# Norming and shifting a feed-forward's input a second time, for its later chunks

## The chip, the cores and the metric

The kernel runs on one core of one Trainium2 chip. The metric is the device time of one execution in microseconds (us). Engines are named as in the profile: PE is TensorE's matmul and PEld its weight load, DVE is VectorE, ACT is ScalarE, POOL is GpSimd, SP is SyncE, which issues the DMAs. DVE and ACT work off their instructions in the order of the program.

## The reference

Two layers, each of three sublayers: a half-step feed-forward network (FFN), a token mixer (attention, Fourier, gMLP), a second half-step FFN. 384 token columns are held: 128 of a prompt and 256 of a sample, each group with its own conditioning vector. What matters here:

```python
def modulate(x, g, shift, scale):
    return rmsnorm(x, g) * (1 + scale) + shift
def swiglu(h, w_in, w_out):
    gate, up = jnp.split(h @ w_in, 2, axis=-1)
    return (jax.nn.silu(gate) * up) @ w_out
# in trunk_layer, for the FFNs 0 and 1:
h = modulate(x, npre[0], mod[:, :, 0], mod[:, :, 1])
x = x + 0.5 * mod[:, :, 2] * rmsnorm(swiglu(h, fw_in[0], fw_out[0]), npost[0])
# mod = silu(c) @ ada_w[l] + ada_b[l], one vector of 9 * 1024 per group (adaLN)
```

D_MODEL is 1024, the FFN's inner width 2816. All tensors are float32.

## The kernel before, in words

Activations lie transposed: 128 features on the partitions, 8 tiles (KT) of 384 columns (T). Every float32 product is made of three matmuls of rounded parts (`mm3`, L176 to L179): high weights with high input, high weights with low input, low weights with high input. Weights are streamed in pieces of 128x1024; ACT rounds a piece to its high part (`whi`, L132), DVE subtracts (`wlo`, L135), five pieces ahead (HOLD).

**An FFN's first product.** 44 *chunks* of 128 rows of `w_in` (22 gates, 22 ups, alternating) are each made by 24 matmuls: 8 input tiles by three. The first chunks of an FFN (6 in the first FFN, 4 in the others) run while the input arrives (`Enter.group`). The others run one after another in the loop at L521; I number these c0, c1, ... A gate and its up are a *pair*. The input is not normed before it is multiplied: the columns hold x times the gain, two more columns (T+2 = 386) hold the shift, and the norm `r` and the shift's share are applied to the result when a chunk leaves PSUM (`biased`, L430; `leave`, L500): per pair DVE copies two columns and multiplies 384 by r for the gate and again for the up, ACT applies Silu with the shift's share as bias on the two groups apart, DVE adds the other bias and multiplies (two instructions, L508), ACT rounds (`ahi`), and POOL subtracts (`alo`, L135).

**Order within the loop.** For each pair: `leave` of the pair before, then for each of its two chunks the split of a weight piece four chunks further on, the chunk's 24 matmuls, and a share of the adaLN products. The rounding of that piece on ACT waits until PE is done with the chunk before, whose buffer it takes.

**adaLN.** The vectors `mod` are made on DVE: one item of `ada_some` is two multiply-and-sum instructions over 1024 columns (L101) and gives 128 of them; 128 items in all. `plan` (L896) says how many of them lie in each FFN's first and second product; before, none lie in the mixes. `Enter.gain` (`A`, L217) of the next sublayer, made while the present one's second product still runs, needs the items of its gain.

**Between sublayers.** `Post.add` squares each finished tile on ACT, POOL adds the squares to `accy`, and PE's sum over partitions (L196) opens the next sublayer. `Enter.begin`, which needs `A`, stands ahead of the second to last of these squares in ACT's order. `Enter.restore` (L421) takes a reciprocal on DVE and brings x to its true scale: on POOL in the FFNs, on POOL and DVE in the mixes.

Of the kernel before, what the change touches and what calls it, by code (L numbers as in the profile page):

```python
# [5 lines left out]
F32 = mybir.dt.float32  # L6
# [6 lines left out]
P = 128  # L13
# [34 lines left out]
def model(nc, tc, a, o):  # L48
# [159 lines left out]
    class Enter:  # L208
# [220 lines left out]

        def biased(self, ps):  # L430
# [63 lines left out]
    def ffn(l, s, post, ada_in, ada_out, enter, after):  # L494
        ps = enter.group()
        with tc.tile_pool(name="ff", bufs=1) as fp:
# [3 lines left out]
            def leave(m, pg, pu):  # L500
                t, bg = enter.biased(pg)
                for j, b, e in RANGES:
                    nc.scalar.activation(t[:, b:e], t[:, b:e], AF.Silu, bias=bg[:, j:j + 1])  # L503
                up, bu = enter.biased(pu)

                def rest():
                    for j, b, e in RANGES:
                        nc.vector.scalar_tensor_tensor(  # L508
                            out=up[:, b:e], in0=up[:, b:e], scalar=bu[:, j:j + 1], in1=t[:, b:e],
                            op0=ALU.add, op1=ALU.mult)  # L510
                    split(ahi[:, m, :], alo[:, m, :], up, nc.gpsimd)

                return rest

            pairs = [(m, ps[2 * m], ps[2 * m + 1]) for m in range(len(ps) // 2)]
            leave(*pairs[0])()
            split_to(at[0] + HOLD - 1)
            for pair in pairs[1:-1]:
                leave(*pair)()
            first = len(pairs)  # L520
            for m in range(first, FT):  # L521
                rest = leave(*pairs[-1])
                for j in range(2):
                    w, = take(between=None if j else rest)
                    p = bank(px if len(ps) == FIRST and enter.post is None else pm)
                    products(p[:, :T + 2], w, enter.parts, range(KT))
                    ps.append(p)
                    if m < FT - REST:
                        ada_some(spread(ada_in, 2 * (m - first) + j, 2 * (FT - REST - first)))
                pairs.append((m, ps[-2], ps[-1]))  # L530
                if first < m <= first + KT:
                    enter.restore([m - first - 1])
            leave(*pairs[-1])()
# [19 lines left out]
    def mix(l, post, enter, after):  # L553
        ps = enter.group()
        with tc.tile_pool(name="mx", bufs=1) as mp, tc.tile_pool(name="m2", bufs=2) as m2:
# [322 lines left out]
            post = Post(l, 1)  # L878
            for i, p in enumerate(outs):
                products(p, w3[i], oparts, [7])  # L880
            enter.restore()
            for m in range(3, KT):
# [7 lines left out]
                outs.append(p)  # L890
                if m == KT - 2:
                    after(post, following)
# [101 lines left out]
```

## Time and profile before

| | |
|---|---|
| three timed runs, median (range) | 1541.15 us (1540.25 to 1542.49) |
| the profiled execution, its own time | 1538.58 us |
| its span | 1536.6 us, so 2.0 us lie around it |
| PE, PEld busy | 1467.3 us (95%), 1418.9 us (92%) |
| DVE, ACT, POOL busy | 1219.7 us (79%), 676.1 us (44%), 420.5 us (27%) |
| granted TensorE clock, mean | 0.991 |

The stages in order, from the span's start: layer 0's first FFN to 317.1 us, the mix to 490.6, the second FFN to 781.3; layer 1's first FFN to 1069.3, its mix to 1228.9, its second FFN to 1520.5, then the output. A matmul's record is longer than the distance from one to the next, since they overlap: rates are read by dividing a stretch by the matmuls in it. "Busy" for PE is therefore no measure of waiting; the idle time in brackets and the time per matmul are.

### The profile page before, as it was taken

How to read it: one execution, taken by the hardware profiler on the slowest of the kernel's cores; microseconds unless marked ns; L12 is line 12 of the kernel's file. 1: busy time of each engine (PE TensorE's matmuls, PEld its weight loads, DVE VectorE, ACT ScalarE, POOL GpSimd, SP SyncE). 2: the span in 40 equal slices, each digit the busy share in tenths (PEclk: the TensorE clock that was granted, in tenths of full speed). 3: DMA queues.
4: the chain of work that ended last, by engine and by line, in shares of the span. 5: the costliest groups of instructions: out<-in, count | busy, mean ns of one | idle time of the engine just before them, and what ended most of it. 6: DMA issues, size and time to landing. Idle time of an engine off the chain costs nothing.

```text
span 1536.6 us, 22588 instructions
## 1 busy us (share of the span) xinstructions
PE 1467.3 (95%) x8412; PEld 1418.9 (92%) x8412; DVE 1219.7 (79%) x2040; ACT 676.1 (44%) x1262; POOL 420.5 (27%) x293
## 2 busy tenths in 40 slices
PE   9999999979889999999999999999989989999996
PEld 7999989978778999999989999999877979999995
DVE  4799999996776899999988999887777789666323
ACT  4533334346655533334344333433667654433331
POOL 1211111124534333121132422111454343311012
PEclk9999999999999999999999999999999999999998
DMA  9566667844333255667835556676244315544441
GB/s 370 192 197 194 203 198 241 260 138 140 97 97 117 87 174 181 200 194 241 259 118 167 177 193 194 204 221 189 91 122 121 102 44 182 174 134 123 119 118 41
DMA packets 87005, 254.12 MB, mean 165 GB/s; under 512 B 21616, under 2 KB 26224, under 8 KB 85872
## 3 DMA queue, kind: packets, MB, share of 16 engines
q1 hardware_dynamic: 86896, 252.68, 51.9%
q8 instruction: 66, 1.08, 0.3%
q14 instruction: 43, 0.35, 0.1%
HBM read 250.03 MB, written 2.62 MB: 164 GB/s over the span
## 4 chain that ended last, share of the span: by engine, by line
PE 56%; DVE 28%; ACT 7%; issue 6%; DMA 2%; POOL 1%; SPq 0%; DVEq 0%; ACTq 0%; POOLq 0%
PE ps L179 17%; PE ps L178 17%; PE ps L177 17%; DVE junk L101 8%; DVE wlo L135 7%; ACT whi L132 3%; DVE hlo L234 2%; DVE x L270 2%; DVE x L268 2%; DVE t L435 1%; DVE p L756 1%; DMA rpb<-in_rpb_dram 1%; PE ps L196 1%; DMA raw<-in_ffn_w_in_dram 1%; ACT t L503 1%
## 5 line engine op out<-in xcount | busy, mean ns | idle before, releaser
L178 PE MATMUL ps<-hlo,whi 128*128 128x386 f32 (+1 forms) x1700 | 579.3, 341 | 11.4 <-DVE hlo L234 10.6
L177 PE MATMUL ps<-hhi,whi 128*128 128x386 f32 (+1 forms) x1700 | 587.1, 345 | 0.8 <-ACT whi L132 0.8
L179 PE MATMUL ps<-hhi,wlo 128*128 128x386 f32 (+1 forms) x1700 | 579.0, 341 | 2.9 <-DVE wlo L135 2.9
L135 DVE TENSOR_TENSOR wlo<-raw,whi 128x1024 fp32r<-128x1024 f32 (+1 forms) x298 | 389.5, 1311 | 171.1 <-ACT whi L132 165.3
L132 ACT CAST whi<-raw 128x1024 fp32r<-128x1024 f32 x324 | 329.9, 1024 | 220.4 <-PE ps L178 144.9
L101 DVE CUSTOM_DVE_ANT_0 junk<-adaw,cb,adab 128x1024 bf16<-128x1024 f32 x256 | 367.4, 1435 | 4.6
L178 PEld LDWEIGHTS ps<-hlo,whi 128*128 128x128 f32 x1700 | 322.8, 190 | 18.7 <-DVE hlo L234 16.8
L177 PEld LDWEIGHTS ps<-hhi,whi 128*128 128x128 f32 x1700 | 322.5, 190 | 6.8 <-issue 2.5
L179 PEld LDWEIGHTS ps<-hhi,wlo 128*128 128x128 f32 x1700 | 322.0, 189 | 6.2 <-DVE wlo L135 6.0
L135 POOL TENSOR_TENSOR alo<-t,ahi 128x384 fp32r<-128x384 f32 x88 | 135.6, 1541 | 513.9 <-ACT ahi L132 513.9
L177 PE MATMUL ps<-ahi,whi 128*128 128x384 f32 x768 | 257.7, 336 | 0.7 <-ACT whi L132 0.7
L179 PE MATMUL ps<-ahi,wlo 128*128 128x384 f32 x768 | 257.1, 335 | 0.6 <-DVE wlo L135 0.6
L178 PE MATMUL ps<-alo,whi 128*128 128x384 f32 x768 | 257.1, 335 | 0.0
L503 ACT ACTIVATE t<-t,b 128x128 f32<-128x128 f32 (+1 forms) x176 | 70.6, 448 | 389.8 <-DVE t L435 389.8
L177 PEld LDWEIGHTS ps<-ahi,whi 128*128 128x128 f32 x768 | 144.3, 188 | 1.3 <-ACT whi L132 1.0
L179 PEld LDWEIGHTS ps<-ahi,wlo 128*128 128x128 f32 x768 | 144.3, 188 | 1.0 <-DVE wlo L135 1.0
L178 PEld LDWEIGHTS ps<-alo,whi 128*128 128x128 f32 x768 | 144.3, 188 | 0.0
L457 POOL TENSOR_TENSOR accy<-accy,sqy 128x384 f32<-128x384 f32 x36 | 54.2, 1506 | 311.0 <-ACT sqy L455 310.9
L435 DVE TENSOR_TENSOR t<-ps,r 128x384 f32<-128x384 f32 x212 | 114.7, 548 | 0.2
L135 POOL TENSOR_TENSOR wlo<-raw,whi 128x1024 fp32r<-128x1024 f32 x26 | 63.2, 2433 | 50.4 <-ACT whi L132 36.2
L508 DVE SCALAR_TENSOR_TENSOR t<-t,b 128x128 f32<-128x128 f32 (+1 forms) x176 | 66.2, 417 | 9.2
L245 POOL TENSOR_TENSOR accx<-accx,sqx 128x384 f32<-128x384 f32 x42 | 46.5, 1107 | 70.3 <-ACT sqx L244 69.0
(167 smaller groups left out, 1146.8 us busy)
## 6 DMA issues: line engine op xcount, KB each, us to landing
raw<-in_ffn_w_in_dram SPq DMA_DIRECT2D x176, 512.0 KB, 3.4
adaw<-in_ada_w_dram SPq DMA_DIRECT2D x128, 512.0 KB, 3.6
raw<-in_ffn_w_out_dram SPq DMA_DIRECT2D x64, 512.0 KB, 3.8
raw<-in_w_in_dram SPq DMA_DIRECT2D x36, 512.0 KB, 4.0
raw<-in_ffn_w_out_dram SPq DMA_DIRECT2D x32, 384.0 KB, 3.7
piece<-in_ada_first_dram SPq DMA_DIRECT2D x8, 1024.0 KB, 8.7
raw<-in_w_out_dram SPq DMA_DIRECT2D x16, 512.0 KB, 3.3
rpb<-in_rpb_dram SPq DMA_DIRECT2D x32, 96.0 KB, 6.3
```

The costliest lines, as they stand in the source:

```text
L101: nc.vector.tensor_tensor_reduce(out=junk, in0=w, in1=cb[:, j, :], scale=1.0, scalar=adab[:, l, b, f:f + 1], op0=ALU.mult, op1=ALU.add, ac ...
L132: nc.scalar.copy(hi, src)
L135: (eng or nc.vector).tensor_tensor(out=lo, in0=src, in1=hi, op=ALU.subtract)
L177: nc.tensor.matmul(ps, whi, hhi, start=start, stop=False)
L178: nc.tensor.matmul(ps, whi, hlo, start=False, stop=False)
L179: nc.tensor.matmul(ps, wlo, hhi, start=False, stop=stop)
L234: nc.vector.scalar_tensor_tensor(out=self.hlo[:, k, b:e], in0=x[:, k, b:e], scalar=self.A[:, k, j:j + 1], in1=self.hhi[:, k, b:e], op0=ALU ...
L245: nc.gpsimd.tensor_tensor(out=self.acc, in0=self.acc, in1=sq, op=ALU.add)
L435: nc.vector.tensor_tensor(out=t, in0=ps[:, :T], in1=self.r, op=ALU.mult)
L457: nc.gpsimd.tensor_tensor(out=self.acc, in0=self.acc, in1=sq, op=ALU.add)
L503: nc.scalar.activation(t[:, b:e], t[:, b:e], AF.Silu, bias=bg[:, j:j + 1])
L508: nc.vector.scalar_tensor_tensor(out=up[:, b:e], in0=up[:, b:e], scalar=bu[:, j:j + 1], in1=t[:, b:e], op0=ALU.add, op1=ALU.mult)
```

## The change

After the first eight chunks (c0 to c7) the input is used in a second form. While these eight run, `normal(k)` is called with each of them: DVE multiplies tile k of x by r, ACT applies gain and shift on the two groups apart and rounds to `nhi`, and DVE subtracts to `nlo`. From c8 on the chunks multiply these parts, with 384 columns, and their pairs leave without norm and bias: ACT makes Silu straight from PSUM, and one DVE instruction multiplies. For all pairs the subtraction `alo` goes from POOL to DVE. The items of adaLN are dealt anew: `plan` gives the FFNs fewer or other numbers, in the first product the first eight calls get a third of the weight of the later ones, and four items lie in each mix (one ahead of the last products with tile 7, one behind each of three output chunks). The room for `nlo` comes from a smaller reserve for DMA descriptors.

```diff
--- before.py
+++ after.py
@@ -427,6 +427,21 @@
                     eng = nc.gpsimd if self.s != 1 or k < 3 else nc.vector
                     eng.tensor_tensor(out=x[:, k, :], in0=x[:, k, :], in1=post.sy, op=ALU.mult)
 
+        def normal(self, k):
+
+            if k == 0:
+                self.nhi = act.tile([P, KT, T], F32R, tag="yg", name="nhi")
+                self.nlo = act.tile([P, KT, T], F32R, tag="nlo", name="nlo")
+                self.nparts = [(self.nhi[:, i, :], self.nlo[:, i, :]) for i in range(KT)]
+            h = tp.tile([P, T], F32, tag="n", bufs=2, name="n")
+            nc.vector.tensor_tensor(out=h, in0=x[:, k, :], in1=self.r, op=ALU.mult)
+            for j, b, e in RANGES:
+                nc.scalar.activation(h[:, b:e], h[:, b:e], AF.Identity, scale=self.A[:, k, j:j + 1],
+                                     bias=mods[self.l, 3 * self.s][:, k, j:j + 1])
+            hi, lo = self.nparts[k]
+            nc.scalar.copy(hi, h)
+            return lambda: nc.vector.tensor_tensor(out=lo, in0=h, in1=hi, op=ALU.subtract)
+
         def biased(self, ps):
 
             t = tp.tile([P, T], F32, tag="t", bufs=3, name="t")
@@ -497,40 +512,69 @@
             ahi = fp.tile([P, FT, T], F32R, name="ahi")
             alo = fp.tile([P, FT, T], F32R, name="alo")
 
-            def leave(m, pg, pu):
-                t, bg = enter.biased(pg)
-                for j, b, e in RANGES:
-                    nc.scalar.activation(t[:, b:e], t[:, b:e], AF.Silu, bias=bg[:, j:j + 1])
-                up, bu = enter.biased(pu)
+            def leave(m, pg, pu, normal):
+
+                if normal:
+                    t = tp.tile([P, T], F32, tag="t", bufs=3, name="t")
+                    up = tp.tile([P, T], F32, tag="t", bufs=3, name="up")
+                    nc.scalar.activation(t, pg[:, :T], AF.Silu)
+                    nc.vector.tensor_tensor(out=up, in0=pu[:, :T], in1=t, op=ALU.mult)
+                else:
+                    t, bg = enter.biased(pg)
+                    for j, b, e in RANGES:
+                        nc.scalar.activation(t[:, b:e], t[:, b:e], AF.Silu, bias=bg[:, j:j + 1])
+                    up, bu = enter.biased(pu)
 
                 def rest():
-                    for j, b, e in RANGES:
-                        nc.vector.scalar_tensor_tensor(
-                            out=up[:, b:e], in0=up[:, b:e], scalar=bu[:, j:j + 1], in1=t[:, b:e],
-                            op0=ALU.add, op1=ALU.mult)
-                    split(ahi[:, m, :], alo[:, m, :], up, nc.gpsimd)
-
-                return rest
-
-            pairs = [(m, ps[2 * m], ps[2 * m + 1]) for m in range(len(ps) // 2)]
-            leave(*pairs[0])()
+                    if not normal:
+                        for j, b, e in RANGES:
+                            nc.vector.scalar_tensor_tensor(
+                                out=up[:, b:e], in0=up[:, b:e], scalar=bu[:, j:j + 1], in1=t[:, b:e],
+                                op0=ALU.add, op1=ALU.mult)
+                    nc.scalar.copy(ahi[:, m, :], up)
+
+                def low():
+                    nc.vector.tensor_tensor(out=alo[:, m, :], in0=up, in1=ahi[:, m, :], op=ALU.subtract)
+
+                return rest, low
+
+            def left(*pair):
+                for f in leave(*pair):
+                    f()
+
+            pairs = [(m, ps[2 * m], ps[2 * m + 1], False) for m in range(len(ps) // 2)]
+            left(*pairs[0])
             split_to(at[0] + HOLD - 1)
             for pair in pairs[1:-1]:
-                leave(*pair)()
+                left(*pair)
             first = len(pairs)
+
+            calls = [1] * KT + [3] * (2 * (FT - REST - first) - KT)
+            shares = [ada_in * sum(calls[:i]) // sum(calls) for i in range(len(calls) + 1)]
             for m in range(first, FT):
-                rest = leave(*pairs[-1])
+                rest, low = leave(*pairs[-1])
                 for j in range(2):
+                    i = 2 * (m - first) + j
                     w, = take(between=None if j else rest)
+                    if j == 0:
+                        low()
+                    lower = enter.normal(i) if i < KT else None
                     p = bank(px if len(ps) == FIRST and enter.post is None else pm)
-                    products(p[:, :T + 2], w, enter.parts, range(KT))
+                    if i < KT:
+                        products(p[:, :T + 2], w, enter.parts, range(KT))
+                    else:
+                        products(p[:, :T], w, enter.nparts, range(KT))
                     ps.append(p)
-                    if m < FT - REST:
-                        ada_some(spread(ada_in, 2 * (m - first) + j, 2 * (FT - REST - first)))
-                pairs.append((m, ps[-2], ps[-1]))
-                if first < m <= first + KT:
-                    enter.restore([m - first - 1])
-            leave(*pairs[-1])()
+                    if i < len(calls):
+                        ada_some(shares[i + 1] - shares[i])
+                    if lower:
+                        lower()
+                        if i:
+                            enter.restore([i - 1])
+                    if i == KT:
+                        enter.restore([KT - 1])
+                pairs.append((m, ps[-2], ps[-1], i >= KT))
+            left(*pairs[-1])
             parts = [(ahi[:, k, :], alo[:, k, :]) for k in range(FT)]
             post = Post(l, s)
             last = None
@@ -876,6 +920,7 @@
                         nc.sync.dma_start(out=o["nv"][l], in_=v[:, 0, :])
                         pair.values()
             post = Post(l, 1)
+            ada_some(1)
             for i, p in enumerate(outs):
                 products(p, w3[i], oparts, [7])
             enter.restore()
@@ -888,12 +933,14 @@
                 products(p, w, oparts, range(2, KT - 1))
                 products(p, w, oparts, [KT - 1])
                 outs.append(p)
+                if m < KT - 2:
+                    ada_some(1)
                 if m == KT - 2:
                     after(post, following)
             post.add(KT - 1, outs[KT - 1])
         return post
 
-    plan = {(0, 0): (26, 22), (0, 2): (20, 20), (1, 0): (18, 14), (1, 2): (8, 0)}
+    plan = {(0, 0): (24, 20), (0, 2): (22, 18), (1, 0): (15, 13), (1, 2): (8, 0)}
     cur, post = Enter(0, 0, None), None
     npost = cst.tile([P, LAYERS * 3, KT], F32, name="npost")
     ident = cst.tile([P, P], F32, name="ident")
@@ -978,7 +1025,7 @@
     import concourse.tile as tile
     from concourse.bass_utils import run_bass_kernel_spmd
 
-    nc = bacc.Bacc("TRN2", target_bir_lowering=False, num_devices=1)
+    nc = bacc.Bacc("TRN2", target_bir_lowering=False, num_devices=1, dynamic_dma_scratch_size=1024)
     z = host(inputs)
     a = {k: nc.dram_tensor(f"in_{k}_dram", v.shape, F32, kind="ExternalInput").ap() for k, v in z.items()}
     o = {k: nc.dram_tensor(f"out_{i}_dram", s, F32, kind="ExternalOutput").ap()
```

How the instructions move, at three places. First DVE in layer 0's second FFN, where the pair after the first two has just left PSUM (t and b of `biased`); before:

```order
L508 SCALAR_TENSOR_TENSOR t<-t,b 128x128
L508 SCALAR_TENSOR_TENSOR t<-t,b 128x256
L135 TENSOR_TENSOR wlo<-raw,whi 128x1024 x2
L101 ISA junk,mod_8_103<-adaw,cb,adab 128x1024
L101 ISA mod_8_103 128x1
L101 ISA junk,mod_8_103<-adaw,cb,adab 128x1024
L101 ISA mod_8_103 128x1
L425 RECIPROCAL sy<-sy 128x384
L434 COPY b<-ps 128x2
```

and now, the same place:

```order
L531 SCALAR_TENSOR_TENSOR t<-t,b 128x128
L531 SCALAR_TENSOR_TENSOR t<-t,b 128x256
L135 TENSOR_TENSOR wlo<-raw,whi 128x1024
L537 TENSOR_TENSOR alo<-t,ahi 128x384
L437 TENSOR_TENSOR n<-x,r 128x384
L443 TENSOR_TENSOR nlo<-n,nhi 128x384
L135 TENSOR_TENSOR wlo<-raw,whi 128x1024
L437 TENSOR_TENSOR n<-x,r 128x384
L443 TENSOR_TENSOR nlo<-n,nhi 128x384
L449 COPY b<-ps 128x2
```

Between two pairs DVE now has `alo` and twice a product `n` with its subtraction `nlo`, and ACT's work on n lies between these two; the adaLN item (four rows junk and mod_8) is gone from here.

Then PE in the ninth chunk of layer 0's first FFN (c8), at tiles 3 and 4 of the input, with the engines that each row waits for; before:

```order
L177 MATMUL ps<-hhi,whi 128x386
L178 MATMUL ps<-hlo,whi 128x386
L179 MATMUL ps<-hhi,wlo 128x386
L177 MATMUL ps<-hhi,whi 128x386
L178 MATMUL ps<-hlo,whi 128x386
L179 MATMUL ps<-hhi,wlo 128x386
```

and now:

```order
L177 MATMUL ps<-nhi,whi 128x384
L178 MATMUL ps<-nlo,whi 128x384
L179 MATMUL ps<-nhi,wlo 128x384
L177 MATMUL ps<-nhi,whi 128x384 [waits Activation_49]
L178 MATMUL ps<-nlo,whi 128x384 [waits DVE_49]
L179 MATMUL ps<-nhi,wlo 128x384
```

The matmuls read nhi and nlo with 384 columns; those of tile 4 wait for ACT (nhi) and DVE (nlo), and so do those of tiles 5, 6 and 7 behind them.

Last DVE in layer 0's mix, from the last head's low part (alo) to the next sublayer's gain A; before:

```order
L135 TENSOR_TENSOR alo<-ps,ahi 128x384
L443 SCALAR_TENSOR_TENSOR gg<-mod_5_100,npost 128x16
L425 RECIPROCAL sy<-sy 128x384
L428 TENSOR_TENSOR x<-x,sy 128x384 x5
L135 TENSOR_TENSOR wlo<-raw,whi 128x1024 x6
L217 SCALAR_TENSOR_TENSOR A<-mod_7_102,npre 128x16
```

and now, from gg on:

```order
L458 SCALAR_TENSOR_TENSOR gg<-mod_5_100,npost 128x16
L101 ISA junk,mod_7_102<-adaw,cb,adab 128x1024
L101 ISA mod_7_102 128x1
L101 ISA junk,mod_7_102<-adaw,cb,adab 128x1024
L101 ISA mod_7_102 128x1
L425 RECIPROCAL sy<-sy 128x384
L428 TENSOR_TENSOR x<-x,sy 128x384 x5
L135 TENSOR_TENSOR wlo<-raw,whi 128x1024 x3
L101 ISA junk,mod_7_102<-adaw,cb,adab 128x1024
L101 ISA mod_7_102 128x1
L101 ISA junk,mod_7_102<-adaw,cb,adab 128x1024
L101 ISA mod_7_102 128x1
```

An adaLN item stands ahead of the reciprocal, and the six weight splits (wlo) ahead of A now have items among them: one behind the third, and one each behind the next two.

## Rows read from the trace of the kernel before

**Rows 1.** Windows, core 0: start:end, length, busy us (count) by engine, PEclk, DMA, GB/s.
```profile
48.60:223.70 175.10, 171.79 (x953) 167.77 (x951) 160.56 (x263) 63.33 (x101) 29.96 (x19) 1.00 0.63 202
223.70:317.10 93.40, 92.08 (x529) 91.43 (x528) 89.75 (x126) 34.19 (x52) 12.10 (x8) 1.00 0.78 250
317.10:328.70 11.60, 6.07 (x18) 4.78 (x17) 8.42 (x14) 6.36 (x13) 3.94 (x3) 0.71 0.68 216
490.58:496.40 5.82, 3.51 (x16) 2.99 (x17) 3.20 (x5) 2.10 (x6) 2.78 (x2) 1.00 0.30 101
517.19:689.80 172.61, 172.41 (x972) 171.95 (x971) 158.40 (x246) 65.00 (x103) 49.33 (x29) 1.00 0.57 183
781.30:784.80 3.50, 3.50 (x17) 2.63 (x16) 2.73 (x5) 1.07 (x2) 1.14 (x1) 1.00 0.80 268
1229.20:1237.00 7.80, 5.15 (x18) 4.24 (x18) 4.15 (x7) 2.45 (x6) 3.70 (x3) 0.78 0.23 79
1256.80:1429.00 172.20, 172.20 (x972) 172.05 (x971) 123.45 (x208) 71.84 (x110) 45.53 (x30) 1.00 0.46 147
1429.00:1520.50 91.50, 91.50 (x529) 91.50 (x529) 24.10 (x25) 28.59 (x44) 10.07 (x7) 1.00 0.32 93
```

**Rows 2.** Timeline of DVE, start of layer 0's second FFN: start, us, instruction, [idle before].
```profile
527.81 0.15 DVE L434 COPY b<-ps 128x2 f32<-128x2 f32 x1
...
535.88 0.15 DVE L434 COPY b<-ps 128x2 f32<-128x2 f32 x1
...
537.13 0.75 DVE L508 SCALAR_TENSOR_TENSOR t<-t,b 128x128 f32<-128x128 f32 x2
...
538.30 3.18 DVE L135 TENSOR_TENSOR wlo<-raw,whi 128x1024 fp32r<-128x1024 f32 x2 [0.42 <-ACT whi L132]
...
543.94 2.55 DVE L425 RECIPROCAL sy<-sy 128x384 f32<-128x384 f32 x1
```

**Rows 3.** Timeline of ACT in the same stretch.
```profile
536.53 0.80 ACT L503 ACTIVATE t<-t,b 128x128 f32<-128x128 f32 x2 [4.96 <-DVE t L435]
...
537.24 1.03 ACT L132 CAST whi<-raw 128x1024 fp32r<-128x1024 f32 x1
...
538.17 0.51 ACT L132 CAST ahi<-t 128x384 fp32r<-128x384 f32 x1
```

**Rows 4.** Timeline of DVE, prices: weight split, adaLN pair of instructions, 384-column SBUF operation.
```profile
304.36 1.22 DVE L135 TENSOR_TENSOR wlo<-raw,whi 128x1024 fp32r<-128x1024 f32 x1
...
305.49 1.28 DVE L101 CUSTOM_DVE_ANT_0 junk<-adaw,cb,adab 128x1024 bf16<-128x1024 f32 x1
...
308.03 0.96 DVE L135 TENSOR_TENSOR wlo<-raw,whi 128x768 fp32r<-128x768 f32 x1
...
788.54 0.56 DVE L270 TENSOR_TENSOR x<-x,yg 128x384 f32<-128x384 f32 x1
```

**Rows 5.** Timeline of DVE, layer 0's first FFN: its third pair, and two late pairs.
```profile
62.82 0.15 DVE L434 COPY b<-ps 128x2 f32<-128x2 f32 x1
...
174.38 0.15 DVE L434 COPY b<-ps 128x2 f32<-128x2 f32 x1
...
192.92 0.16 DVE L434 COPY b<-ps 128x2 f32<-128x2 f32 x1
```

**Rows 6.** Timelines of DVE and PE where the two FFNs of layer 0 end.
```profile
317.76 0.17 DVE L217 SCALAR_TENSOR_TENSOR A<-mod,npre 128x16 f32<-128x16 f32 x1
...
322.66 1.65 PE L196 MATMUL ps<-accy,ones 128*128 128x384 f32 x2 [5.53 <-POOL accy L457]
...
775.04 0.17 DVE L217 SCALAR_TENSOR_TENSOR A<-mod,npre 128x16 f32<-128x16 f32 x1
```

**Rows 7.** Windows of the two mixes' output projections, same columns as Rows 1.
```profile
467.30:488.16 20.86, 20.86 (x122) 20.86 (x120) 17.20 (x15) 13.51 (x26) 12.06 (x8) 1.00 0.38 123
1205.94:1227.14 21.20, 21.20 (x124) 21.20 (x123) 17.20 (x15) 13.51 (x26) 12.04 (x8) 1.00 0.39 127
```

**Rows 8.** Timeline of DVE at the first mix's end.
```profile
487.18 0.98 DVE L217 SCALAR_TENSOR_TENSOR A<-mod,npre 128x16 f32<-128x16 f32 x1
```

## The prediction

> **What bounds the kernel now.** I read the busy time and the clock by stage first, then the timelines of DVE and ACT where the changed loop begins, then the ends of the sublayers.
>
> By stage, PE has work all the time in the long products: layer 1's second FFN gives 172.20 us for 972 matmuls, nearly all with 386 columns, or 177.2 ns each; its second product, with 384 columns, 91.50 us for 529, or 173.0 ns [rows 1]. The granted clock is 1.00 in both, the 2.4 GHz level. Such stretches end when PE is through, and a faster DVE gains nothing there.
>
> Two things are bound by DVE. Layer 0's first FFN: its first product takes 175.10 us for 953 matmuls, 6.2 us more than 953 x 177.2 ns, and the second begins with 93.40 us for 529, 1.9 us more than at 173.0 ns [rows 1]. There two pairs take DVE 18.54 us from copy to copy [rows 5], and PE 96 x 0.1772 = 17.0. DVE is still behind when this FFN ends: A comes at 317.76, 0.7 us after PE's last product at 317.1, and PE stands 5.53 us for accy; after layer 0's second FFN A comes at 775.04, 6.3 us ahead of PE's end at 781.3, and PE stands for nothing [rows 6]. The ends cost 11.60 us against 3.50 [rows 1]: 8.1 us more, 5.5 of them idle and the rest a granted clock of 0.71, of which part is at the 1.2 GHz level, after that idle time.
>
> The other places are the mixes' ends: 5.82 us at the first, of which 3.50 is work and so 2.3 idle at full clock, and 7.80 us at the second at a clock of 0.78 [rows 1].
>
> **The change part by part.** *Columns.* From c8 on, 30 chunks in the first FFN and 32 in each of the others have 24 matmuls with 384 columns: 720 and 768 matmuls x (177.2 - 173.0) ns = 3.0 and 3.2 us, together -12.7 us. The gap between the two rates may come in part from the 386-column pitch of the old tiles; the new ones have that of the second product's, so I take all of it (bounds 0 and 4.6 ns, the latter from layer 0's second FFN, 172.61 us for 972 [rows 1]).
>
> By the Trainium skill, page "TensorE: Matmul & The Clock Gate", section "Back-to-back issue gap", an isolated warm matmul takes its columns at 2.4 GHz plus a constant, so two columns are 0.83 ns; an estimate from that is 2.5 us in place of 12.7. The two rates of this trace are 4.2 ns apart and speak against it.
>
> *Making the second parts.* This is the largest term, and it is a new wait. c8 can't end before nlo of tile 7, and DVE makes that last, behind everything else of the four pairs. I add up one pair's round on DVE as it now stands, each price from a row. From the copy to the start of the first weight split 2.42 us (535.88 to 538.30, the 0.42 of waiting for ACT's rounding included) [rows 2]; that split 1.13 (304.36 to 305.49) [rows 4]; alo 0.56 and n 0.56, at the price of a 384-column operation on SBUF [rows 4]. Then DVE must wait, since the next in its order is nlo: ACT takes 0.80 for two groups and 0.51 to round [rows 3], with 0.04 from one engine to the other (the rounding ends at 538.27, the split that waits for it begins at 538.30 [rows 2, 3]) 1.35 in all. Then nlo 0.56; the second weight piece's rounding, 1.03 on ACT behind that of n [rows 3], ends 0.45 after nlo; the split 1.13, n 0.56, ACT 1.35, nlo 0.56. Together 10.6 us a round, where PE needs 48 x 0.1776 = 8.5.
>
> In layer 0's second FFN the first such round begins at 527.81 [rows 2], as before. Four rounds are 42.5 us, the reciprocal of sy between the first and the second 2.55 [rows 2]; one adaLN item, 2.54 us (305.49 to 308.03) [rows 4], stands between an n and its nlo and hides 1.35 of waiting, so +1.2. nlo of tile 7 is there at 574.1. PE would reach it at: 9 matmuls of the group and 8 x 24 after 517.19, at 177.6 ns [rows 1], c8 begins at 552.9, and 22 matmuls later it is 556.7. PE stands 17.4 us in all, in four pieces (tiles 4 to 7). Before, nothing of this was waited for, and DVE's lag of 9 us at c0 (518.8) had five weight pieces and two free pairs of banks to spend; they are not long enough now, since the wait is for data that only this order yields.
>
> The same holds for layer 1's first FFN (one item there too, 17.4) and its second (none, 16.2). Layer 0's first FFN has no reciprocal of sy; its loop's rounds begin at 62.82 [rows 5], about 1.1 later now for one alo and the wait ahead of it, so at 63.9; with two items nlo of tile 7 comes at 63.9 + 42.5 + 2.4 = 108.8, and PE reaches it at 48.60 + 231 x 0.1772 + 3.8 = 93.3: 15.5 us. The bounds of the round are 9.3 (ACT's steps half overlapped) and 12 us (POOL's restore slowing DVE), which is 5 us a stage either way. I take 10.6, the plain sum.
>
> After pieces of standing of some 4 us each PE starts cold. The two ends with a clock below 1.00 cost 11.60 - 3.50 - 5.5 = 2.6 and 7.80 - 3.50 - 2.65 = 1.65 us beyond their idle time, the 5.82 one nothing [rows 1]: I take 2.0 a stage, bounds 0 and 2.6.
>
> *After c8.* Per pair DVE has one multiplication, one alo, two splits and the items; in layer 0's first FFN, with 24 x 12/86 = 3.35 items for two pairs, 4 x 0.56 + 4 x 1.13 + 3.35 x 2.54 = 15.3 us and perhaps 1 of waiting, against 16.6 for PE. POOL no longer works beside it. So the 8.1 us of stalls there go, and with 20 items in its second product, as many as layer 0's second FFN had, A is early enough and the 8.1 us at the end go too. What is late next is PE itself.
>
> *Items in the mixes.* Four items, 10.2 us, come onto DVE between gg and A. DVE is idle 20.86 - 17.20 = 3.7 us of that stretch in the first mix and 4.0 in the second [rows 7], and A itself, 0.98 beside POOL [rows 8], falls to 0.17 [rows 6]. A comes 10.2 - 3.7 - 0.8 = 5.7 and 5.4 us later, and PE waits already for what hangs on it (ACT's square, POOL's accy), so all of it is on the path. At the first the clock falls too, +1.6; the second has that already. Queued behind the items are the reciprocal of sy, the restore on DVE and POOL, the weight splits and, through their buffers, SP's loads; nothing of them is late before A is. Bounds 0 and 9 us each. The descriptor reserve I cost at nothing: all large transfers are issued by SP, and none is waited for here; no row prices it.
>
> **The sum**, from the profiled execution's 1538.6 us. Layer 0's first FFN: 15.5 + 2.0 - 3.0 - 8.1 - 8.1 = -1.7. Its second and layer 1's first: 17.4 + 2.0 - 3.2 = +16.2 each. Layer 1's second: 16.2 + 2.0 - 3.2 = +15.0. Mixes: 5.7 + 1.6 + 5.4 = +12.7. Together +58.4, so 1597.0; the runs' median lies 2.6 above the profiled execution, so 1599.6, say **1600 us**.
>
> **The rivals.** *A: the parts are ready in time,* at the four switches to c8. For this a round must take no more than (556.7 - 527.81 - 2.55)/4 = 6.6 us [rows 1, 2]; below that the wait is gone. It would come if ACT's share between n and nlo did not hold DVE up, and the Silu, split and restore were quicker than their rows. Then 66.5 us of standing and 8.0 of clock fall away: 58.4 - 74.5 = -16, 1525 us, faster. For it: DVE kept up before with a round of 8.1 us (527.81 to 535.88), one item included. Against it: the order of DVE leaves nothing to do between n and nlo, and the rows give 10.6.
>
> *B: the items in the mixes are hidden.* If what waits there is not A, 12.7 us fall away: 1587. For it, DVE's idle time ahead of the last alo; against it, the items come after that alo.
>
> *C: columns give only what their number says,* the rule named above, as a mechanism that the 4.2 ns are a property of the stage and stay: 3024 matmuls then gain 2.5 or less, and the time is 1610. The two products of one FFN, both at full clock, speak against it.
>
> *D: the switch binds, but half,* because the rounds begin earlier (the alo of POOL no longer slows the splits) and take 9 us: standing 11 us a stage, 1574.
>
> **How the numbers follow.** The forecast 0.60, A 0.17, B 0.08, C 0.05, D 0.10. The forecast's own range is 1578 to 1620: the round's bounds, about 20 us either way over four stages, with the mixes' and the clock's beside it. B, C and D lie within 1568 to 1620, which I give for 8 in 10; A is left out below it. What a measurement of this kernel can tell from no change is about 0.2%, 3 us. Faster by more is A, 0.17; slower by more is the rest but for 0.02, so 0.81; within it 0.02.
>
> **What would show it.** In the changed kernel's trace: PE idle in the ninth chunk, waiting for DVE's nlo at tiles 4 to 7, some 17 us in each FFN; DVE idle some 1.35 us ahead of each nlo, waiting for nhi; rounds of 10.6 us. No stalls later in layer 0's first FFN, and 3.5 us at its end. Mix ends of 12 to 13 us. Rates of 173 ns from c9 on. The forecast is wrong if PE passes c8 without idle time, which shows in that chunk alone, and its size is wrong if the rounds are not 10.6.

## The result, and the profile after

The changed kernel takes 1611.6 us (median of 4 runs, 1610.3 to 1614.4) against 1540.7 us for the kernel before in the same runs: ratio 1.0463, 95% interval 1.0444 to 1.0482, so slower, by 70.9 us. Forecast were 1600 us and a range of 1568 to 1620. The profiled execution has a span of 1608.5 us, 71.9 more than before. By stage, from the first matmul of one sublayer's group phase to that of the next, changes in us:

| stage | forecast | measured |
|---|---|---|
| start and layer 0's first FFN | -1.7 | -1.3 |
| layer 0's mix | +7.3 | +9.7 |
| layer 0's second FFN | +16.2 | +17.1 |
| layer 1's first FFN | +16.2 | +16.7 |
| layer 1's mix | +5.4 | +13.2 |
| layer 1's second FFN, end | +15.0 | +16.5 |
| together | +58.4 | +71.9 |

The windows of the changed kernel, columns as in [rows 1]: start:end, length, PE, PEld, DVE, ACT, POOL busy, granted clock, DMA.

```profile
89.20:232.40 143.20, 131.04 (x724) 127.75 (x723) 119.05 (x177) 55.09 (x80) 0.00 (x0) 0.94 0.64 205
130.00:230.00 100.00, 100.00 (x579) 100.00 (x578) 84.65 (x121) 35.57 (x48) 0.00 (x0) 1.00 0.71 224
240.00:320.00 80.00, 80.00 (x463) 80.00 (x463) 75.43 (x103) 30.73 (x49) 7.82 (x6) 1.00 0.80 253
323.90:327.40 3.50, 3.50 (x17) 2.62 (x17) 2.05 (x4) 1.07 (x2) 1.19 (x1) 1.00 0.45 153
563.10:715.30 152.20, 139.26 (x770) 136.09 (x771) 121.07 (x177) 58.50 (x85) 4.96 (x4) 0.94 0.62 197
806.80:810.30 3.50, 3.50 (x17) 2.62 (x17) 2.06 (x4) 1.07 (x2) 1.20 (x1) 1.00 0.44 150
868.60:1020.00 151.40, 138.51 (x770) 135.28 (x771) 103.95 (x149) 58.77 (x85) 4.98 (x4) 0.94 0.54 173
1350.00:1500.80 150.80, 138.81 (x769) 135.66 (x770) 87.55 (x121) 57.58 (x85) 4.01 (x4) 0.94 0.43 139
```

The four long lines are the stretches from c8 to the end of each first product. Their 720 and 768 matmuls would take 124.6 and 132.9 us at 173.0 ns; they take 143.2, 152.2, 151.4 and 150.8, or 74.3 us more in all, at a mean clock of 0.94. Away from c8 the same product runs at full clock. A window also counts matmuls that only reach into it, so its 579 in 100 us look like 172.7 ns; from one start to the next it is 173.4 ns, against 177.2 for the chunks with 386 columns and 173.3 for the second product, in both kernels. The ends of layer 0's FFNs take 3.50 us both, against 11.60 and 3.50 there.

One round on DVE in layer 0's first FFN (start, length, instruction, [idle before, and what ended it]), which answers to [rows 2]:

```profile
63.38 0.15 DVE L449 COPY b<-ps 128x2 f32<-128x2 f32 x1
...
67.47 0.55 DVE L437 TENSOR_TENSOR n<-x,r 128x384 f32<-128x384 f32 x1
...
69.63 0.56 DVE L443 TENSOR_TENSOR nlo<-n,nhi 128x384 fp32r<-128x384 f32 x1 [1.60 <-ACT nhi L442]
...
70.58 1.23 DVE L135 TENSOR_TENSOR wlo<-raw,whi 128x1024 fp32r<-128x1024 f32 x1 [0.40 <-ACT whi L132]
...
73.88 0.56 DVE L443 TENSOR_TENSOR nlo<-n,nhi 128x384 fp32r<-128x384 f32 x1 [1.60 <-ACT nhi L442]
...
74.35 0.15 DVE L449 COPY b<-ps 128x2 f32<-128x2 f32 x1
...
108.28 0.56 DVE L443 TENSOR_TENSOR nlo<-n,nhi 128x384 fp32r<-128x384 f32 x1
```

From copy to copy it is 10.97 us. Twice DVE stands 1.60 us for nhi ahead of nlo, and 0.40 for whi; with 0.45 ahead of the round's other weight split that is 4.05 us of waiting. The last line is nlo of tile 7, there at 108.84. ACT in the same round, beside [rows 3]:

```profile
68.06 0.99 ACT L439 ACTIVATE n<-n,mod,A 128x128 f32<-128x128 f32 x2 [1.82 <-DVE n L437]
...
69.08 0.51 ACT L442 CAST nhi<-n 128x384 fp32r<-128x384 f32 x1
...
69.50 1.05 ACT L132 CAST whi<-raw 128x1024 fp32r<-128x1024 f32 x1
```

ACT begins n's two activations when DVE has made n (67.47 to 68.03), rounds nhi, and only then the next weight piece: all of it comes between two instructions of DVE that wait for it. On PE c8 shows the wait, piece by piece, and what follows it:

```profile
92.32 0.44 PE L177 MATMUL ps<-nhi,whi 128*128 128x384 f32 x1 [0.47 <-ACT nhi L442]
...
96.56 0.64 PE L177 MATMUL ps<-nhi,whi 128*128 128x384 f32 x1 [3.03 <-ACT nhi L442]
...
103.21 0.69 PE L177 MATMUL ps<-nhi,whi 128*128 128x384 f32 x1 [5.05 <-ACT nhi L442]
...
107.44 0.69 PE L177 MATMUL ps<-nhi,whi 128*128 128x384 f32 x1 [2.63 <-ACT nhi L442]
...
108.89 0.69 PE L178 MATMUL ps<-nlo,whi 128*128 128x384 f32 x1 [0.76 <-DVE nlo L443]
...
109.37 0.52 PE L179 MATMUL ps<-nhi,wlo 128*128 128x384 f32 x1
...
109.69 0.52 PE L177 MATMUL ps<-nhi,whi 128*128 128x384 f32 x1
```

PE stands 0.47, 3.03, 5.05 and 2.63 us for nhi of tiles 4 to 7, and 0.76 for the last nlo; from 109.37 its matmuls start every 0.32 us, the 1.2 GHz level, until 113.5.

At layer 0's mix end: the window from gg, DVE's instruction just ahead of the first item, to the end of A, beside the first of [rows 7], then DVE and PE, beside [rows 8]; the last line is PE in the kernel before:

```profile
466.71:495.15 28.44, 23.57 (x134) 22.92 (x132) 28.27 (x31) 13.52 (x26) 10.48 (x8) 1.00 0.46 152
```

```profile
466.71 0.17 DVE L458 SCALAR_TENSOR_TENSOR gg<-mod,npost 128x16 f32<-128x16 f32 x1
...
485.44 2.04 DVE L101 CUSTOM_DVE_ANT_0 junk<-adaw,cb,adab 128x1024 bf16<-128x1024 f32 x1
...
487.52 1.92 DVE L101 CUSTOM_DVE_ANT_0 junk<-adaw,cb,adab 128x1024 bf16<-128x1024 f32 x1
...
489.37 2.02 DVE L135 TENSOR_TENSOR wlo<-raw,whi 128x1024 fp32r<-128x1024 f32 x1
...
494.98 0.17 DVE L217 SCALAR_TENSOR_TENSOR A<-mod,npre 128x16 f32<-128x16 f32 x1
```

```profile
479.64 0.45 PE L179 MATMUL ps<-hhi,wlo 128*128 128x384 f32 x1 [1.84 <-DVE wlo L135]
...
499.87 1.65 PE L196 MATMUL ps<-accy,ones 128*128 128x384 f32 x2 [7.74 <-POOL accy L472]
```

```profile
492.89 0.91 PE L196 MATMUL ps<-accy,ones 128*128 128x384 f32 x2 [2.31 <-POOL accy L457]
```

From gg to the end of A it is 28.44 us, of which DVE works 28.27; before it was 20.86, with 3.66 idle [rows 7]. PE stands 1.84 us for a weight split, which it did not before, and 7.74 instead of 2.31 us for accy. Its sum over partitions comes 33.16 us after gg, before 25.60: 7.56 later, and 7.24 later in layer 1's mix. An item's instruction beside POOL takes 2.04 or 1.92 us where it takes 1.28 alone [rows 4].

### The profile page after: what moved, and what is told of

The parts are those of the page before. It is cut to its first block, busy times and chain, and to the rows that moved or that the text cites. A ratio compares the mean times of both kernels' runs of the same rounds, so it can differ in the third digit from the quotient of the medians.

```text
span 1608.5 us, 22400 instructions
## 1 busy us (share of the span) xinstructions
PE 1480.7 (92%) x8412; PEld 1420.6 (88%) x8412; DVE 1163.8 (72%) x1877; ACT 712.3 (44%) x1295; POOL 264.2 (16%) x205
## 4 chain that ended last, share of the span: by engine, by line
PE 63%; DVE 21%; ACT 8%; DMA 3%; issue 3%; POOL 2%; SPq 1%; DVEq 0%; POOLq 0%; ACTq 0%
PE ps L178 20%; PE ps L179 20%; PE ps L177 20%; DVE wlo L135 4%; ACT whi L132 3%; DVE hlo L234 2%; DMA rpb<-in_rpb_dram 2%; ACT n L439 2%; DVE x L270 2%; DVE x L268 2%; DVE t L450 1%; DVE junk L101 1%; PE ps L196 1%; DVE n L437 1%; POOL wlo L135 1%
## 5 line engine op out<-in xcount | busy, mean ns | idle before, releaser
L177 PE MATMUL ps<-nhi,whi 128*128 128x384 f32 x1008 | 344.3, 342 | 46.1 <-ACT nhi L442 43.8
L178 PE MATMUL ps<-nlo,whi 128*128 128x384 f32 x1008 | 343.9, 341 | 4.2 <-DVE nlo L443 4.2
L179 PE MATMUL ps<-nhi,wlo 128*128 128x384 f32 x1008 | 341.9, 339 | 2.0 <-DVE wlo L135 1.9
L178 PE MATMUL ps<-hlo,whi 128*128 128x386 f32 (+1 forms) x692 | 238.8, 345 | 11.4 <-DVE hlo L234 10.6
L177 PE MATMUL ps<-hhi,whi 128*128 128x386 f32 (+1 forms) x692 | 245.3, 354 | 0.0
L179 PE MATMUL ps<-hhi,wlo 128*128 128x386 f32 (+1 forms) x692 | 237.8, 344 | 4.5 <-DVE wlo L135 4.5
L177 PEld LDWEIGHTS ps<-nhi,whi 128*128 128x128 f32 x1008 | 192.8, 191 | 53.7 <-ACT nhi L442 50.4
L178 PEld LDWEIGHTS ps<-nlo,whi 128*128 128x128 f32 x1008 | 192.5, 191 | 9.1 <-DVE nlo L443 9.1
L179 PEld LDWEIGHTS ps<-nhi,wlo 128*128 128x128 f32 x1008 | 192.8, 191 | 3.3 <-DVE wlo L135 3.3
L178 PEld LDWEIGHTS ps<-hlo,whi 128*128 128x128 f32 x692 | 132.7, 192 | 18.6 <-DVE hlo L234 16.7
```

Of the source, the lines that this page charges most:

```text
L177: nc.tensor.matmul(ps, whi, hhi, start=start, stop=False)
L178: nc.tensor.matmul(ps, whi, hlo, start=False, stop=False)
L179: nc.tensor.matmul(ps, wlo, hhi, start=False, stop=stop)
```

## The experiments

Times are medians; ratios are to the kernel before in the same runs, with 95% intervals.

**The switch at c12.**

```diff
+SWITCH = 12
...
-                    if i < KT:
+                    if i < SWITCH:
                         products(p[:, :T + 2], w, enter.parts, range(KT))
...
-                pairs.append((m, ps[-2], ps[-1], i >= KT))
+                pairs.append((m, ps[-2], ps[-1], i >= SWITCH))
```

> The second parts are read from the thirteenth chunk of the loop on (c12), not from c8; they are made as early as in the changed kernel. Theory, the wait for nlo of tile 7: PE, which does not stand, reaches tile 7 of c12 17.0 us (96 x 0.1772) later than that of c8, at 110.0 us in layer 0's first FFN, where nlo of tile 7 was there at 108.8. The 74.3 us by which the four stretches from c8 on (143.2, 152.2, 151.4 and 150.8 us) are longer than their 720 and 768 matmuls at 173.0 ns all go; four chunks go back to 177.2 ns, 1.6 us in all. 1611.6 - 74.3 + 1.6 = 1539 us. Rival, DVE is short of time in any case: the backlog then falls on weight splits and free PSUM banks in c8 to c11 and half of the loss stays, 1576 us.

1569.2 us, ratio 1.0174 (1.0149 to 1.0199). PE no longer waits for nlo, and 42.4 us come back, which shows that this wait was the largest loss. But they are 42, not 74. PE in layer 0's second FFN of this kernel (its line numbers are one higher):

```profile
556.67 0.44 PE L178 MATMUL ps<-hhi,whi 128*128 128x386 f32 x1 [0.78 <-ACT whi L133]
...
563.65 0.45 PE L180 MATMUL ps<-hhi,wlo 128*128 128x386 f32 x1 [1.20 <-DVE wlo L136]
...
568.58 0.44 PE L178 MATMUL ps<-hhi,whi 128*128 128x386 f32 x1 [0.78 <-ACT whi L133]
```

The wait has gone over to weight pieces, in c7 to c14. With rounds of 11 us against PE's 8.5, DVE falls behind whichever data PE reads; the rival (1576 us) came nearer than the theory (1539).

**nlo one tile late.**

```diff
+            lowers = []
...
                     if lower:
-                        lower()
+                        lowers.append(lower)
+                        if i:
+                            lowers.pop(0)()
+                        if i == KT - 1:
+                            lowers.pop(0)()
```

> One order on DVE is changed: nlo of tile i is issued behind n of tile i + 1 (tile 7's where it stood), so ACT has a chunk's time for nhi. Theory, the ping-pong between DVE and ACT makes the round long: two waits of 1.6 us a round go, the round falls from 10.97 to about 7.8 us, under PE's 8.5; four rounds from 63.4 with two items (2 x 1.2) give tile 7 at about 97 us, where PE is due at 93: 2 to 6 us of standing in each stage instead of 18 to 19; some 1560 us (1545 to 1580). Rival, DVE's own work makes the round long and ACT's share is hidden beside it: the round stays above 10 us and the time above 1600 us.

1596.6 us, ratio 1.0351 (1.0330 to 1.0371): near the rival's number, but not for its reason. DVE in this kernel, two copies that are a round apart, and the weight split ahead of the second:

```profile
65.55 0.15 DVE L449 COPY b<-ps 128x2 f32<-128x2 f32 x1
...
72.75 1.23 DVE L135 TENSOR_TENSOR wlo<-raw,whi 128x1024 fp32r<-128x1024 f32 x1 [2.55 <-ACT whi L132]
...
74.83 0.15 DVE L449 COPY b<-ps 128x2 f32<-128x2 f32 x1
```

The round fell only to 9.28 us. The idle time ahead of nlo is gone, and 2.55 us ahead of one weight split have taken its place: ACT's rounding of the weight piece stands behind n's activations, which wait for DVE. My first theory, that nlo's place alone made the round long, fell; the next run shows that DVE's own work was not the limit either.

**Both orders.** As before, and n is issued ahead of the split's subtraction (it goes into the split's `between`, behind the rounding of the weight piece):

```diff
-                    w, = take(between=None if j else rest)
+                    made = []
+                    def between():
+                        if j == 0:
+                            rest()
+                        if i < KT:
+                            made.append(enter.normal(i))
+                    w, = take(between=between)
...
-                    lower = enter.normal(i) if i < KT else None
+                    lower = made[0] if made else None
```

> As in the second experiment nlo is issued one tile late; besides, n of a chunk is issued ahead of the weight split's subtraction, so that ACT rounds the weight piece first and n's parts behind it. The switch stays at c8. Theory, changed after the second experiment: the round was long because DVE and ACT waited for each other in turn, with nlo late it was the weight piece's rounding that stood behind n's two activations (2.07 us of waiting ahead of one wlo in each round, round 9.2 to 9.3 us). Now both waits have cover: the round is DVE's own work, some 7 us without an item; nlo of tile 7 comes at 63.4 + 4 x 7.0 + 2 x 2.56 = 96.5 us in layer 0's first FFN, PE is due at 93; 3 to 5 us of standing and 1 to 2 of clock in each stage instead of 18 to 19: 1611.6 - 4 x 13 = 1559 us (1550 to 1575). Rival, ACT or DVE has no room whatever the order: the round stays at 9 us or more and the time near the second experiment's 1597 us.

1571.6 us (1566.5 to 1577.0), ratio 1.0182 (1.0149 to 1.0214); 12 above the forecast of it, inside its range. The profiled execution took 1577.0. Copies of two rounds without an item in layer 0's first FFN, and the last nlo:

```profile
65.60 0.15 DVE L449 COPY b<-ps 128x2 f32<-128x2 f32 x1
...
72.50 0.16 DVE L449 COPY b<-ps 128x2 f32<-128x2 f32 x1
...
81.88 0.15 DVE L449 COPY b<-ps 128x2 f32<-128x2 f32 x1
...
88.72 0.15 DVE L449 COPY b<-ps 128x2 f32<-128x2 f32 x1
...
97.62 1.02 DVE L443 TENSOR_TENSOR nlo<-n,nhi 128x384 fp32r<-128x384 f32 x2
```

The round is 6.90 and 6.84 us, 4.1 less than in the changed kernel with the same arithmetic: those 4.1 us were waiting. From c8 to the end of the first product PE loses 6.7 us against 173.0 ns a matmul, 3.3 of them standing, where it lost 18.6; in the other three FFNs 12.3, 12.2 and 9.3. There the reciprocal of sy comes on top, which I had left out.

**No item in the first eight chunks**, on top of this:

```diff
-            calls = [1] * KT + [3] * (2 * (FT - REST - first) - KT)
+            calls = [0] * KT + [3] * (2 * (FT - REST - first) - KT)
```

> The kernel of the new order (run e5_order, 1571.6 us) with no adaLN item in the first eight chunks; switch at c8, items in the mixes. Theory: what is left of the wait is made by the items (two in layer 0's first FFN, one in each of the two next, 2.56 us each) and by the reciprocal of sy (2.55). Layer 0's first FFN has no reciprocal: its 3.8 us of standing and 1.5 of clock go; the next two lose 2.6 each of their 9.1 us; layer 1's second has no item there and keeps its 6.9. 1571.6 - 5.3 - 5.2 - 2 of clock = 1559 us (1553 to 1564). Rival, DVE's order of rounds and not the items makes the rest: 1571 us.

1561.4 us, ratio 1.0131 (1.0107 to 1.0155). Layer 0's first FFN from c8 on:

```profile
91.80:216.70 124.90, 124.90 (x722) 124.90 (x721) 112.09 (x164) 46.69 (x65) 0.00 (x0) 1.00 0.72 230
```

The clock stays at 1.00 and PE does not stand; 9.3, 9.1 and 8.5 us are left in the other FFNs. Where one item went, 12.3 fell to 9.3 and 12.2 to 9.1: at the switch an item costs some 3 us, about its own 2.5 on DVE. What is left is not the reciprocal of sy (2.55) alone. A round in layer 0's second FFN:

```profile
540.37 0.15 DVE L449 COPY b<-ps 128x2 f32<-128x2 f32 x1
...
547.43 1.37 DVE L443 TENSOR_TENSOR nlo<-n,nhi 128x384 fp32r<-128x384 f32 x1
...
548.72 0.15 DVE L449 COPY b<-ps 128x2 f32<-128x2 f32 x1
```

```profile
546.45 1.93 POOL L428 TENSOR_TENSOR x<-x,sy 128x384 f32<-128x384 f32 x1 [1.55 <-DVE n L437]
```

It takes 8.35 us, not 6.9. POOL's restore of x, which layer 0's first FFN does not have, runs beside two of DVE's subtractions in each round, and these take 1.35 to 1.38 us each where they take 0.55 alone. In the changed kernel the restore fell mostly into DVE's waits.

**The items out of the mixes.**

```diff
             post = Post(l, 1)
-            ada_some(1)
...
-                if m < KT - 2:
-                    ada_some(1)
...
-    plan = {(0, 0): (24, 20), (0, 2): (22, 18), (1, 0): (15, 13), (1, 2): (8, 0)}
+    plan = {(0, 0): (26, 22), (0, 2): (20, 20), (1, 0): (18, 14), (1, 2): (8, 0)}
```

> The eight adaLN items go back from the mixes to the FFNs, as they were before ((26, 22), (20, 20), (18, 14), (8, 0)); the rest is the changed kernel. Theory, the items delay A at the mixes' ends and nothing else does: the mixes take 328.7 -> 496.4 and 164.2 us again, 22.9 us less than in the changed kernel (177.4 twice), and 1611.6 - 22.9 = 1589 us; if the 10 us beyond the forecast of 12.7 come from another part of the change (later loads of rpb, the descriptor reserve) or from chance, 1599 us. With 26 and 22 items layer 0's first FFN may end late again: 0 to 8 us on top. Rival, the mixes' loss is none of the items': no change, 1611 us.

1595.4 us, ratio 1.0340 (1.0318 to 1.0362): 16.2 less, between the two figures. Layer 0's first FFN still ends in 3.5 us, with 26 and 22 items: what mended that end in the changed kernel is not the plan alone. Here PE's standing at c8 also gives DVE time; the run with all edits, below, ends the same without it.

**The items alone, in the kernel before** (the edit above the other way round).

> The kernel before with the items alone: four in each mix, and the changed plan (24, 20), (22, 18), (15, 13), (8, 0). Theory, as forecast: +5.7 and +5.4 us at the mixes' ends, 1.6 of clock, and up to 8.1 us less at the end of layer 0's first FFN, whose plan has four items fewer: 1545 to 1553 us. If the items are the whole loss of the mixes (22.9 us): 1555 to 1563 us. Rival, they are hidden: 1533 to 1541 us.

1549.3 us (1546.0 to 1555.1), ratio 1.0058 (1.0039 to 1.0077). The profiled execution took 1554.9. The first FFN of this kernel, product and end:

```profile
48.50:219.00 170.50, 169.58 (x953) 168.41 (x951) 156.30 (x255) 63.70 (x101) 29.94 (x19) 1.00 0.62 202
312.00:316.40 4.40, 3.84 (x18) 2.94 (x18) 4.26 (x6) 2.02 (x4) 1.54 (x2) 1.00 0.79 248
```

The product takes 4.6 us less than in [rows 1] and the end 4.40 instead of 11.60, though POOL makes alo as before: four items fewer are enough as well. The mixes lose more than this gains. That the time lies in the theory's range is partly luck: in this execution layer 0's first FFN took 12.3 us less than before, not 8.1, and the mixes 26.7 more, not 12.7.

**The descriptor reserve alone**, in the kernel before.

```diff
-    nc = bacc.Bacc("TRN2", target_bir_lowering=False, num_devices=1)
+    nc = bacc.Bacc("TRN2", target_bir_lowering=False, num_devices=1, dynamic_dma_scratch_size=1024)
```

> The kernel before with the smaller descriptor reserve alone. The mixes' first parts, where no item was added, take 115.3 and 113.0 us from the group's first product to the end of the third later projection in the changed kernel (115.0 and 113.1 in the third experiment, without items), and 110.6 and 108.2 before. Theory, the reserve has no part in it: 1540 us, within 0.2%, and 110.6 and 108.2 us. Rival, the reserve makes rpb land later: 115 and 113 us, 1549 us.

1540.7 us, ratio 0.9994 (0.9978 to 1.0010): it costs nothing that can be measured here. The mixes' first parts (up to the last matmul with 386 columns) took 110.9 and 113.1 us in its profiled execution, so even this near copy of the kernel before shows 113 once.

**The tiles' pitch.** The changed kernel with the new tiles as wide as the old ones; the products are the same.

```diff
-                self.nhi = act.tile([P, KT, T], F32R, tag="yg", name="nhi")
-                self.nlo = act.tile([P, KT, T], F32R, tag="nlo", name="nlo")
-                self.nparts = [(self.nhi[:, i, :], self.nlo[:, i, :]) for i in range(KT)]
+                self.nhi = act.tile([P, KT, T + 2], F32R, tag="yg", name="nhi")
+                self.nlo = act.tile([P, KT, T + 2], F32R, tag="nlo", name="nlo")
+                self.nparts = [(self.nhi[:, i, :T], self.nlo[:, i, :T]) for i in range(KT)]
```

> The changed kernel, with nhi and nlo laid out with a pitch of 386 columns, of which 384 are read. Theory, the two columns themselves make the difference between 177.2 and 173.0 ns a matmul: 173.0 ns behind c12, as in the changed kernel. Rival, the pitch does: 177 ns there. The total is the changed kernel's, or up to 12 us more.

1621.9 us (one run). Windows of the first and of the second product of layer 0's first FFN:

```profile
130.00:230.00 100.00, 100.00 (x573) 100.00 (x572) 84.38 (x121) 35.30 (x48) 0.00 (x0) 1.00 0.71 224
240.00:320.00 80.00, 80.00 (x456) 80.00 (x456) 75.73 (x104) 30.14 (x49) 7.01 (x6) 1.00 0.80 253
```

From one start to the next the first product's matmuls take 175.3 ns, between the two theories (173.4 in the changed kernel). And the second product, whose tiles kept their pitch, is slower too: 176.0 ns where the changed kernel has 173.3 (456 and 463 matmuls in the same 80 us). Both hold in all four FFNs, while c0 to c7 run at 177.1 in both kernels. So where a tile lies counts beside its columns; how the difference between 177.2 and 173.4 ns divides is not settled.

**All together**: both orders, the switch at c10, no item in the first eight chunks, none in the mixes (the edits above).

> All together: the order of the run before, the switch at c10 in place of c8, no adaLN item in the first eight chunks (the later ones have them), no items in the mixes and the plan of before. Theory: no standing is left at the switch; of the changed kernel's 1611.6 us the 78 of standing and clock in c0 to c8 and behind and the 16.2 that the third experiment gave go, two chunks at 177.2 ns cost 0.8: 1518 us (1512 to 1535), faster than before. Rival, DVE's backlog turns up as weight splits that come late in c8 to c12: 1535 to 1550 us.

1516.4 us (1515.8 to 1518.7), ratio 0.9838 (0.9818 to 0.9857): 24 us faster than the kernel before, and 95 faster than the changed one; forecast were 1518. Its first product behind the switch, the end of this FFN, and the product of layer 0's second FFN:

```profile
99.90:216.60 116.70, 116.70 (x675) 116.70 (x675) 110.18 (x164) 41.06 (x58) 0.00 (x0) 1.00 0.75 243
308.10:311.60 3.50, 3.50 (x17) 2.62 (x17) 2.41 (x5) 1.07 (x2) 1.21 (x1) 1.00 0.84 235
546.80:671.80 125.00, 125.00 (x723) 125.00 (x723) 106.72 (x157) 47.89 (x68) 0.93 (x1) 1.00 0.68 218
```

PE is busy throughout at full clock: the 672 matmuls from c10 on take 116.48 us, 173.3 ns each, and no FFN has a stall from c0 on. Of the 22.5 us by which this execution is shorter than the one before the change, layer 0's first FFN gives 17.1 and each other FFN about 3; the mixes take 3.5 more.

**The same with the items in the mixes** and the changed plan.

> The run with all edits (e6_all, 1516.4 us), but with the eight items in the mixes and the changed plan. It prices these items without any standing in the FFNs. By the stretch from a mix's third later projection to its end (55.7 us on average in the kernels without items, 65.2 in those with them) they cost 9.5 us a mix: 1516.4 + 19 = 1535 us. By the forecast's price (12.7): 1529 us. Rival, the loss in the mixes went with the late FFNs: 1516 us.

1532.5 us, ratio 0.9952 (0.9938 to 0.9965): the items cost 16.1 us, as in the changed kernel (16.2), so this price does not hang on the FFNs.

## Why the prediction was right, point by point

*Columns.* Forecast 4.2 ns each, measured 3.8 from start to start (177.2 to 173.4); the 173.0 ns of the forecast, read from a window, was 173.3. Rival C is out as a time. Its rule, by which two columns fewer are an estimated 2.5 us in all (the Trainium skill, "TensorE: Matmul & The Clock Gate", "Back-to-back issue gap"), can't be tested on this change alone, since the new tiles also lie elsewhere: at the old pitch the gain was 1.9 ns.

*The wait for nlo of tile 7.* Right, in place and size. The round was 10.97 us against 10.6: ACT's two activations of n, with scale and bias by pointer, took 0.99 where I had put the Silu's 0.80, which have a bias alone. By the Trainium skill ("ScalarE: Activation LUTs", "What ACT_TABLE_LOAD costs") each such pointer adds about 93 ns; for the two activations that is an estimated 0.19, and the rows show 0.19. nlo of tile 7 came at 108.84 (forecast 108.8) and in layer 0's second FFN 78.7 us after the stage's start (77.7). That the first agrees to 0.1 us is luck: the rounds began 0.5 us earlier than forecast, four of them took 1.4 longer, and the two items cost 0.8 less. Loss from c8 on 18.6, 19.3, 18.5 and 17.9 us, with the clock, against 17.5, 19.4, 19.4 and 18.2. The division was off: less idle time (12.1 us of 18.6 in the first) and more half-speed work between the pieces. Another 1.7 us ahead of c8 in three FFNs (37.6 us for the 201 matmuls up to it, 35.9 before) went to late weight pieces, which I had thought covered.

*Why the round is long.* The prediction put it on the empty place between n and nlo. The two runs on the order show that this is half of it: the queue on ACT counts as much, and only with both turned is the round DVE's own work, 6.9 us in layer 0's first FFN and 8.35 in layer 0's second, beside POOL.

*After c8.* Right: no stalls, ends of 3.50 us. The runs give two sufficient causes, fewer items (the items alone: an end of 4.40 us) or the new arithmetic (all together, with 26 and 22 items: 3.50), where I had named both together.

*Items in the mixes.* Forecast 12.7, measured 16.1 and 16.2. The mechanism was right, DVE's queue ahead of A, but the step "A comes 10.2 - 3.7 - 0.8 = 5.7 and 5.4 us later" was too small: from gg to the end of A it is 7.6 us more in the first mix, and PE's sum comes 7.56 and 7.24 later, 3.7 more than forecast in all. DVE's idle time went as forecast. But the four items took 11.4 us instead of 10.2, since one of them ran beside POOL, and the restore of x on DVE 0.8 more. "Nothing of them is late before A is" was wrong too: the first item stands ahead of the reciprocal of sy, the split behind it comes late, and PE waits 1.84 and 1.87 us for it. By the trace this costs nothing more: DVE has no idle time up to A, and PE would have waited for accy instead.

*What is left* of the 12 us between 1600 and 1611.6 (13.5 by the profiled executions): some 3 in the FFNs, and the rest in the mixes. These took 22.9 us more in the profiled execution: 14.8 from gg to the sum and 1.9 behind it, where the clock is lower (1.6 in the forecast), 9.5 in their first parts, less 3.3 between the two. The first parts, where nothing was changed, took 115.3 and 113.0 us (110.6 and 108.2 before). In layer 0's mix PE stood 4.86 us at one wait for softmax's p (1.82 before), and the clock fell to 0.50 after it. The trace leads that wait back over DVE, which stood 3.41 us for POOL's bias (0.98 before), to the loads of rpb, which SP issued 2.1 us later in the mix. This part took 110.6 and 110.9 us in the kernel before and with the reserve alone, and 112.8 to 115.3 in all the others, those with the items alone and those with the new arithmetic alone; so it seems to go with the edits there, and it is not the reserve. In layer 1's mix no edit goes with it: 108.2 before, 113.1 with the reserve alone, 108.6 to 113.2 in the others. Why SP issues later stays open.

*The rivals.* A, with rounds under 6.6 us in layer 0's second FFN, did not come, and the better order has 8.35 there. In layer 0's first FFN, which has no reciprocal, the same condition is (93.3 - 63.9)/4 = 7.35 us; the better order without items has 6.9 there, and PE did not stand. B is out by the runs with and without the items. D is out by the round; its standing of 11 us a stage was near the 12 to 13 seen, but not its loss, since the clock adds to it.

## What to carry to other kernels

When a change makes data on two engines in turn, write both queues down before adding up durations: each hand-over costs the whole share of the other engine unless something independent stands there, on both queues. Turning the order was worth 40 us here at unchanged arithmetic, as much as moving the reader four chunks back. Then look at what else runs where the waits were: POOL's restore had been hidden in them. And let the reader of new data switch over when the last piece is due, not when the last piece is issued; extra work in such a stretch is paid in full.

## What the runs showed of the hardware

A matmul of 384 columns at full clock took 173.3 to 176.0 ns from start to start for the same code: the last figure is the second product's after two other tiles had grown by two columns a row, and nothing but the place of tiles in SBUF had changed for it. DVE's instruction for an item went from 1.28 to 2.04 us, and a weight split from 1.22 to 2.02, where POOL added to accy beside it:

```profile
484.54 1.86 POOL L472 TENSOR_TENSOR accy<-accy,sqy 128x384 f32<-128x384 f32 x1 [6.04 <-ACT sqy L470]
...
487.28 1.08 POOL L472 TENSOR_TENSOR accy<-accy,sqy 128x384 f32<-128x384 f32 x1 [0.88 <-ACT sqy L470]
...
489.23 1.08 POOL L472 TENSOR_TENSOR accy<-accy,sqy 128x384 f32<-128x384 f32 x1 [0.88 <-ACT sqy L470]
```

The first two fall into the two instructions of the slow item, the third into the slow weight split shown above. A subtraction of 384 columns went from 0.55 to 1.37 us beside POOL's restore of x, in the round shown with the run without items in the first eight chunks.
